# Seven modulation vectors: from plain fp32 matmuls on TensorE to sums of scaled weight rows on VectorE

## The chip, the cores and the metric

The kernel runs on one core of a Trainium2 chip. The metric is device time in microseconds (us). Before the change three runs gave a median of 3255.69 us (3248.14 to 3256.19). One further run was taken with the hardware profiler; all rows below come from it.

## The reference, cut to what matters

Two token groups, 256 context tokens and 1024 latent tokens, go through a trunk of two layers (an even mixer with attention and a linear recurrence, an odd mixer with Fourier and long-convolution branches), each followed by an MLP. Every layer is modulated by six vectors of 1024 numbers per group, which depend on a conditioning vector alone:

```
m = silu(cvec) @ mod_w[l] + mod_b[l]            # mod_w[l]: 1024 x 6144, cvec: c_ctx (context) or c (latent)
mp, ms = the six slices of m for c_ctx and for c
h = rmsnorm(x) * (1 + m[1]) + m[0];   x = x + m[2] * mixer(h)
h = rmsnorm(x) * (1 + m[4]) + m[3];   x = x + m[5] * mlp(h)      # mlp: square(relu(h @ w1)) @ w2
```

So there are 2 x 6 modulation vectors, each a product of a 2 x 1024 matrix (both groups) with a 1024 x 1024 slice of `mod_w`. All arithmetic is fp32; products that need it are built from a high and a low fp32r part of each factor (three matmuls for one).

## The kernel before, in words

Activations lie feature-major: 128 features on the partitions, 1280 tokens (256 context, 1024 latent) on the free axis, eight such tiles. The stages run one after the other: filter generation with the first modulation vectors, even mixer (projection, recurrence, attention), output projection, first MLP, odd input projection (`odd_in`), the two convolution passes (`hyena`) with the Fourier branch between, output projection, second MLP. The program is written as generators that are pulled into one another; the tile framework then orders each engine's instructions by a simulated timeline and sets the waits. Each engine works through its own list in order.

The MLP (`mlp`, L778) is a seven-product block scheme. In its first half 16 hidden tiles `j` are made; each takes seven products (`product`, L826: 24 matmuls of 128x128 by 128x320 into a pair of PSUM banks) named 11, T1, T2, 21, T3, 22, T4. Several products accumulate onto the same bank pair, and between them ScalarE copies the partial result (L855, L915, L917) or VectorE adds it to another tile (L859, L921, L925). VectorE and ScalarE split each weight tile into its high and low part (`wtile`, L794: cast on ScalarE, subtraction on VectorE, L295 inside the helper `sub`), GpSimd forms sums of weight blocks (`wset`, L806), and results go to DRAM over the SyncE queue (`keep`, L846). At the end of each hidden tile the MLP pulls its filler four times (L938). The second half (L1007 on) reads the results back and multiplies by the second weights.

Five of the twelve vectors are made outside the first MLP or not touched by the change: `modulation_pe` makes vectors 1, 0, 2, 4 and 3 of layer 0 earlier in the program. The other seven, vector 5 of layer 0 and all six of layer 1, are the filler of the first MLP (`fill2`, L1951) and are made by `modulation` (L357). For one vector it runs eight steps. A step loads two tiles `mw` of 128 x 512 fp32 over the SyncE queue (L368) and issues four matmuls (L371), each with 128x32 of the silu vector as the stationary side and 256 weight columns as the moving one, into four different groups of 32 PSUM partitions. After four steps ScalarE copies the bank to `ms` (L375). After eight, eight matmuls with a selection matrix (L379) add the four partition groups and transpose, and VectorE adds the bias (L380). An fp32 matmul stands in the trace as two records. `modulation` also yields after each step, so 63 pulls finish it within the 64 of the MLP.

Vectors 1 and 0 of layer 1 are needed for the norm in front of the odd input projection, vector 5 of layer 0 at the end of the first MLP, and vectors 2, 4, 3, 5 of layer 1 only in the output projection and the second MLP.

`odd_in` (L1468) makes 16 output tiles `i`. Each loads one weight tile over the SyncE queue (`wload`, L665: load, cast `wh` on ScalarE, subtraction `wl` on VectorE), runs 72 matmuls (`proj`, L673), scales by the norm on VectorE (`evac`, L698) and, for 12 of them, runs a three-tap convolution (one ScalarE and two VectorE passes, L1501 and L1503); 12 tiles are transposed on TensorE.

The pool `tp` holds a ring of 128 x 512 fp32 temporaries that `tmp` (L244) hands out: `mw`, `ms`, the weight sums `s1` of the MLPs, `ub` and `dg` of the projection, `win` of the filter generation, `r1` and `r2` of the rotary embedding.

## Time and profile before

| | |
|---|---|
| median of three runs | 3255.69 us |
| profiled execution | 3253.46 us |
| its span on the core | 3251.3 us |
| TensorE busy | 91% of the span |
| VectorE busy | 59% |
| ScalarE, GpSimd busy | 40%, 31% |
| granted TensorE clock, mean | 0.952 of full speed |

The span is what the trace covers; the execution is 2.2 us longer. The first half of the first MLP lies at about 781 to 1291 us, its second half up to 1702 us, the odd input projection from 1711 us to about 1945 us, and the second MLP begins at 2378 us. PE stands for TensorE, DVE for VectorE, ACT for ScalarE, POOL for GpSimd, SP for SyncE.

### The profile page before, as it was taken

To read this page: it belongs to the slowest core of one execution; us is meant where nothing else is said; L and a number is where in the kernel's file an instruction comes from. 1 tells how busy PE (TensorE), PEld (TensorE's weight loads), DVE (VectorE), ACT (ScalarE), POOL (GpSimd) and SP (SyncE) were. 2 spreads that over 40 slices of the span, in tenths; PEclk is the share of its full clock that TensorE was granted. 3 is DMA by queue.
4 is the path that set the end of the run, shared out by engine and by line. 5 is a ranking of instruction groups with operands and counts; after the bars stand their busy time and mean duration, and the time that the engine had idled before them with its cause. 6 is when DMAs were issued, how large, how long until landed. Compare 5 with 4: busy or idle time off the path is not lost. (4 is left out here: it accounts for less than half of the span.)

```text
span 3251.3 us, 47128 instructions
## 1 busy us (share of the span) xinstructions
PE 2973.1 (91%) x18846; PEld 2718.9 (84%) x18846; DVE 1914.1 (59%) x2266; ACT 1286.9 (40%) x1960; POOL 1010.6 (31%) x674
## 2 busy tenths in 40 slices
PE   6689978898899999999989997887969999999997
PEld 3577767787789988999988885667969999999997
DVE  6986788747644434554664338686585444455465
ACT  5565757733423333333343332232343333333332
POOL 3530045423332222130340015453143333222043
PEclk8799989999899999999999998888989999999998
DMA  7372332252455557785541234555413333775554
GB/s 240 106 244 90 117 122 85 72 209 82 149 175 180 182 177 268 249 288 170 172 174 41 73 99 149 198 161 187 147 63 124 140 136 134 254 265 206 192 193 138
DMA packets 177679, 524.49 MB, mean 161 GB/s; under 512 B 19810, under 2 KB 34546, under 8 KB 177460
## 3 DMA queue, kind: packets, MB, share of 16 engines
q1 hardware_dynamic: 165940, 479.54, 42.6%
q0 software_dynamic: 11520, 41.95, 4.3%
q8 instruction: 148, 2.42, 0.3%
q14 instruction: 71, 0.58, 0.1%
HBM read 392.68 MB, written 128.74 MB: 160 GB/s over the span
## 5 line engine op out<-in xcount | busy, mean ns | idle before, releaser
L1024 PE MATMUL pd<-oh,wt 128*128 128x320 f32 x3584 | 681.2, 311 | 19.1 <-ACT wt L298 8.8
L1024 PEld LDWEIGHTS pd<-oh,wt 128*128 128x128 f32 x3584 | 565.8, 189 | 25.1 <-ACT wt L298 13.2
L831 PE MATMUL pd<-BT,wt 128*128 128x320 f32 x3072 | 483.7, 313 | 12.3 <-DVE BT L761 12.2
L831 PEld LDWEIGHTS pd<-BT,wt 128*128 128x128 f32 x3072 | 459.7, 190 | 31.4 <-issue 18.1
L1024 PE MATMUL pd<-ol,wt 128*128 128x320 f32 x1792 | 410.6, 310 | 1.5 <-DVE ol L295 1.5
L295 DVE TENSOR_TENSOR wt<-wr,wt 128x512 fp32r<-128x512 f32 (+1 forms) x256 | 230.3, 901 | 301.8 <-ACT wt L797 273.7
L831 PE MATMUL pd<-B,wt 128*128 128x320 f32 x2304 | 371.8, 316 | 29.6 <-DVE u L859 17.2
L831 PEld LDWEIGHTS pd<-B,wt 128*128 128x128 f32 x2304 | 351.8, 193 | 42.2 <-DVE u L859 17.8
L295 DVE TENSOR_TENSOR ol<-ur,oh 128x1280 fp32r<-128x1280 f32 x112 | 195.1, 1743 | 246.3 <-PE pd L1024 200.5
L1024 PEld LDWEIGHTS pd<-ol,wt 128*128 128x128 f32 x1792 | 302.3, 189 | 1.9 <-DVE ol L295 1.8
L298 ACT CAST oh<-ur 128x1280 fp32r<-128x1280 f32 x112 | 141.4, 1263 | 339.4 <-DMA ur<-uscr 336.3
L684 PE MATMUL pb<-hh,wh 128*128 128x258 f32 (+1 forms) x720 | 189.7, 367 | 8.0 <-DVE xm L988 8.0
L684 PE MATMUL pb<-hl,wh 128*128 128x258 f32 (+1 forms) x720 | 195.7, 372 | 0.0
L684 PE MATMUL pb<-hh,wl 128*128 128x258 f32 (+1 forms) x720 | 191.8, 370 | 0.0
L797 ACT CAST wt<-wr 128x512 fp32r<-128x512 f32 x192 | 118.7, 620 | 170.9 <-PE pd L831 145.8
L684 PEld LDWEIGHTS pb<-hh,wh 128*128 128x128 f32 x720 | 122.5, 192 | 33.4 <-issue 13.0
L684 PEld LDWEIGHTS pb<-hl,wh 128*128 128x128 f32 x720 | 123.0, 191 | 26.3 <-issue 6.7
L684 PEld LDWEIGHTS pb<-hh,wl 128*128 128x128 f32 x720 | 122.7, 192 | 26.1 <-issue 5.8
L810 POOL TENSOR_TENSOR s<-wr 128x512 f32<-128x512 f32 x32 | 42.3, 1322 | 325.9 <-DMA wr<-in_w_dram 283.7
L306 PE MATMUL pb<-arh,tab 128*128 128x512 f32 x288 | 115.3, 426 | 25.6 <-ACT arh L298 16.2
L298 ACT CAST wh<-wr 128x1024 fp32r<-128x1024 f32 x62 | 64.9, 1048 | 158.8 <-PE pd L684 88.2
L298 ACT CAST wt<-wr 128x1024 fp32r<-128x1024 f32 x64 | 67.3, 1052 | 112.3 <-PE pd L1024 100.9
(529 smaller groups left out, 5588.2 us busy)
## 6 DMA issues: line engine op xcount, KB each, us to landing
wr<-in_w_dram SPq DMA_DIRECT2D x196, 512.0 KB, 3.7
uscr<-u SPq DMA_DIRECT2D x224, 320.0 KB, 2.4
ur<-uscr SPq DMA_DIRECT2D x112, 640.0 KB, 4.2
tab<-in_dft_dram POOLq DMA_DIRECT2D x79, 512.0 KB, 4.8
mw<-in_mw_dram SPq DMA_DIRECT2D x112, 256.0 KB, 4.3
wq<-in_w_dram SPq DMA_DIRECT2D x48, 512.0 KB, 6.2
mw<-in_mw_dram SPq DMA_DIRECT2D x40, 512.0 KB, 5.0
x<-in_x_dram SPq DMA_DIRECT2D x16, 640.0 KB, 7.7
```

Source lines behind the costliest of these rows:

```text
L295: eng.tensor_tensor(o, x, y, ALU.subtract)
L298: S.copy(hi, src)
L306: T.matmul(ps, w, m, start=(i == 0), stop=(i == n - 1))
L684: T.matmul(ps[c][:, 0:N], w[wi][:, sl], hs[k][hi][:, c0:c0 + N], start=(ki == 0 and pi == 0), stop=(ki == nk - 1 and pi == 2))
L797: S.copy(t[:, 0], src)
L810: G.tensor_tensor(s1, a21, a22, ALU.add)
L831: T.matmul(ps[:, c, 0:NQ], w[:, wi, 128 * k:128 * k + 128], B[n][k][:, hi_, NQ * c:NQ * c + NQ], start=(onto is None and k == 0 and pi == ...
L1024: T.matmul(ps[mi][:, z, 0:NQ], w[wi][:, k2, 128 * mi:128 * mi + 128], o[oi][:, k2, NQ * z:NQ * z + NQ], start=(fresh and kk == 0 and k2 == ...
```

## The change

`modulation` no longer runs the weights through TensorE. For one vector it takes two halves of 512 columns. For a half it loads eight tiles `mq` of 128 x 512 (128 rows of the weight matrix each), and for each tile and each of the two groups VectorE multiplies the tile by one number per partition (the silu value of that row) and adds it to an accumulator `macc` of 128 x 2 x 512. The first tile of a half writes the accumulator (a tensor_scalar), the other seven add (scalar_tensor_tensor). At the end of a half eight matmuls with `macc` as the stationary side and one column of ones as the moving one sum over the partitions and bring the result feature-major; VectorE adds the bias. A vector has 18 yields.

Three vectors (layer 0's 5, layer 1's 1 and 0) stay in the first MLP; the other four (layer 1's 2, 4, 3, 5) become the filler of `odd_in`, which pulls five times per output tile. The ring of temporaries shrinks from 6 to 4. The weights are packed accordingly.

```diff
-    o["mw"] = mw.reshape(2, 2, 4, 128, 24, 256).transpose(0, 4, 1, 3, 2, 5).reshape(2, 24, 2, 128, 1024)
+    o["mw"] = mw[0, :, 0:5120].reshape(2, 4, 128, 20, 256).transpose(3, 0, 2, 1, 4).reshape(20, 2, 128, 1024)
+    o["mq"] = np.concatenate([mw[0, :, 5120:], mw[1]], axis=1).reshape(8, 128, 7, 2, 512).transpose(2, 3, 0, 1, 4)
...
-    tp = root.enter_context(tc.tile_pool(name="tp", bufs=6))
+    tp = root.enter_context(tc.tile_pool(name="tp", bufs=4))
...
     def modulation(l, which):
         for i in which:
-            mss = []
-            for jj in range(2):
-                ps = tbank()
-                for h in range(2):
-                    for kk in range(2):
-                        ws = []
-                        for z in range(2):
-                            w = tmp("mw", (128, 2, 256))
-                            ld(w.rearrange("p k c -> p (k c)"), a["mw"][l, 4 * i + 2 * jj + h, kk, :, 512 * z:512 * z + 512])
-                            ws.append(w)
-                        for g in range(4):
-                            T.matmul(ps[32 * g:32 * g + 32, 256 * h:256 * h + 256], st[:, 4 * kk + g, :], ws[g // 2][:, g % 2, :],
-                                     start=kk == 0, stop=kk == 1)
-                        yield
-                ms = tmp("ms")
-                S.copy(ms, ps)
-                mss.append(ms)
-            p2 = tbank()
-            for c in range(8):
-                T.matmul(p2[:, 2 * c:2 * c + 2], mss[c // 4][:, 128 * (c % 4):128 * (c % 4) + 128], sel, start=True, stop=True)
-            V.tensor_tensor(mod[l][i], p2[:, 0:16].rearrange("p (c s) -> p c s", s=2),
-                            mb[:, l, 8 * i:8 * i + 8].unsqueeze(2).to_broadcast([128, 8, 2]), ALU.add)
-            yield
+            for hf in range(2):
+                acc = cp.tile([128, 2, 512], F32, tag="macc", name="macc")
+                for k in range(8):
+                    w = tmp("mq")
+                    ld(w, a["mq"][i + 1 if l else 0, hf, k])
+                    for z in range(2):
+                        if k:
+                            V.scalar_tensor_tensor(acc[:, z], w, st[:, k, z:z + 1], acc[:, z], ALU.mult, ALU.add)
+                        else:
+                            V.tensor_scalar(acc[:, z], w, st[:, k, z:z + 1], None, ALU.mult)
+                    yield
+                p2 = tbank()
+                for c in range(4):
+                    for z in range(2):
+                        T.matmul(p2[:, 2 * c + z:2 * c + z + 1], acc[:, z, 128 * c:128 * c + 128], ones[:, 0:1], start=True, stop=True)
+                V.tensor_tensor(mod[l][i][:, 4 * hf:4 * hf + 4, :], p2[:, 0:8].rearrange("p (c s) -> p c s", s=2),
+                                mb[:, l, 8 * i + 4 * hf:8 * i + 4 * hf + 4].unsqueeze(2).to_broadcast([128, 4, 2]), ALU.add)
+                yield
...
         for i in list(range(8)) + list(range(12, 16)) + list(range(8, 12)):
...
             ps = proj(w, 0, 128, hs, HC, order=[4, 5, 6, 7, 0, 1, 2, 3])
+            pull(filler, 5)
...
         def fill2():
             yield from modulation(0, (5,))
-            yield from modulation(1, (1, 0, 2, 4, 3, 5))
+            yield from modulation(1, (1, 0))
...
-        odd_in(n2, norm_end(n2), vt, h0)
+        fill = modulation(1, (2, 4, 3, 5))
+        odd_in(n2, norm_end(n2), vt, h0, fill)
+        drain(fill)
```

The changed file has four lines less ahead of the MLP, so its L827 is L831 of before, L368 and L370 are the new accumulations, L375 the new column sums and L376 the bias. The engines' lists move as follows.

First TensorE in the first half of the first MLP, around the place where a hidden tile's product 22 (operands `B_6875` to `B_6899`) and T4 (`BT_6878` to `BT_6902`) end and the next tile begins. Before:

```order
L831 MATMUL pd<-B_6899,wt 128x320 x6
L371 MATMUL pt<-mw,silu 32x256 x2
L831 MATMUL pd<-BT_6878,wt 128x320 x6
L831 MATMUL pd<-BT_6886,wt 128x320 x6
L831 MATMUL pd<-BT_6894,wt 128x320 x6
L831 MATMUL pd<-BT_6902,wt 128x320 x6
L371 MATMUL pt<-mw,silu 32x256 x2
L379 MATMUL pt<-c_sel,ms 128x2 x4
L831 MATMUL pd<-B_6276,wt 128x320 x6
```

And at the same place now:

```order
L827 MATMUL pd<-B_6899,wt 128x320 x6
L827 MATMUL pd<-B_6276,wt 128x320 x3
L375 MATMUL pt<-ones,macc 128x1
L827 MATMUL pd<-B_6276,wt 128x320 x3
L375 MATMUL pt<-ones,macc 128x1 x3
L827 MATMUL pd<-BT_6878,wt 128x320 x6
L827 MATMUL pd<-BT_6886,wt 128x320 x6
L827 MATMUL pd<-BT_6894,wt 128x320 x6
L827 MATMUL pd<-BT_6902,wt 128x320 x6
L375 MATMUL pt<-ones,macc 128x1 x4
```

The `mw` matmuls are gone from the list, and six times in this half of the MLP (14 times in all) eight column sums over `macc` stand among the products.

Then VectorE for one hidden tile of the same half (from the addition L859 on, L855 in the changed file). Before:

```order
L859 TENSOR_TENSOR u_8368<-u_8368,pd 128x640
L295 TENSOR_TENSOR wt<-wr,wt 128x512
L921 TENSOR_TENSOR u_8398<-u_8398,pd 128x640
L295 TENSOR_TENSOR wt<-s_8523,wt 128x512
L922 SCALAR_TENSOR_TENSOR u_8398<-u_8398 128x640
L925 TENSOR_TENSOR u_8368<-u_8368,pd 128x640
L295 TENSOR_TENSOR wt<-wr,wt 128x512
L926 SCALAR_TENSOR_TENSOR u_8368<-u_8368 128x640
L295 TENSOR_TENSOR u_8368<-u_8368 128x640
L295 TENSOR_TENSOR u_8398<-u_8398,u_8368 128x640
```

And now:

```order
L855 TENSOR_TENSOR u_8267<-u_8267,pd 128x640
L296 TENSOR_TENSOR wt<-wr,wt 128x512
L368 SCALAR_TENSOR_TENSOR macc<-mq,silu,macc 128x512 x2
L917 TENSOR_TENSOR u_8297<-u_8297,pd 128x640
L368 SCALAR_TENSOR_TENSOR macc<-mq,silu,macc 128x512
L296 TENSOR_TENSOR wt<-s_8422,wt 128x512
L368 SCALAR_TENSOR_TENSOR macc<-mq,silu,macc 128x512
L918 SCALAR_TENSOR_TENSOR u_8297<-u_8297 128x640
L921 TENSOR_TENSOR u_8267<-u_8267,pd 128x640
L296 TENSOR_TENSOR wt<-wr,wt 128x512
L922 SCALAR_TENSOR_TENSOR u_8267<-u_8267 128x640
L296 TENSOR_TENSOR u_8267<-u_8267 128x640
```

The accumulations stand singly and in pairs in front of and between the additions from PSUM (L917, L921) and the weight splits.

Last VectorE for one output tile of the odd input projection (L698 scales by the norm, L1503 is the convolution, `wl` the low part of the next weights; L694, L1500 and L296 in the changed file). Before:

```order
L698 TENSOR_TENSOR xp<-pb,R 128x512 x2
L295 TENSOR_TENSOR wl<-wr,wh 128x1024
L698 TENSOR_TENSOR xp<-pb,R 128x256
L1503 SCALAR_TENSOR_TENSOR u<-xp,hy_14657,u 128x1024
L1503 SCALAR_TENSOR_TENSOR u<-xp,hy_14657,u 128x256
```

And now:

```order
L694 TENSOR_TENSOR xp<-pb,R 128x512 x2
L368 SCALAR_TENSOR_TENSOR macc<-mq,silu,macc 128x512
L296 TENSOR_TENSOR wl<-wr,wh 128x1024
L694 TENSOR_TENSOR xp<-pb,R 128x256
L368 SCALAR_TENSOR_TENSOR macc<-mq,silu,macc 128x512 x3
L1500 SCALAR_TENSOR_TENSOR u<-xp,hy_14355,u 128x1024
L1500 SCALAR_TENSOR_TENSOR u<-xp,hy_14355,u 128x256
L1500 SCALAR_TENSOR_TENSOR u<-xp,hy_14355,u 128x1024
L1500 SCALAR_TENSOR_TENSOR u<-xp,hy_14355,u 128x256
L368 SCALAR_TENSOR_TENSOR macc<-mq,silu,macc 128x512 x8
```

Up to eight accumulations in a row now fill the place between the convolution of one tile and the scaling of the next.

## Rows read from the trace of the kernel before

**Rows 1.** The page: span, and busy time of the engines.

```profile
span 3251.3 us, 47128 instructions
PE 2973.1 (91%) x18846; PEld 2718.9 (84%) x18846; DVE 1914.1 (59%) x2266; ACT 1286.9 (40%) x1960; POOL 1010.6 (31%) x674
```

**Rows 2.** Windows: stretch, length, busy PE PEld DVE ACT POOL, clock, DMA share, GB/s.

```profile
840.00:1300.00 460.00, 456.40 (x3142) 408.65 (x3143) 187.37 (x236) 143.90 (x229) 135.39 (x92) 0.99 0.57 195
980.00:1130.00 150.00, 150.00 (x1051) 136.63 (x1050) 60.97 (x75) 48.37 (x79) 43.13 (x30) 1.00 0.53 180
1720.00:1920.00 200.00, 200.00 (x1079) 171.10 (x1078) 65.62 (x88) 69.65 (x114) 2.10 (x28) 1.00 0.20 60
2500.00:2600.00 100.00, 100.00 (x683) 100.00 (x682) 47.78 (x57) 35.32 (x56) 35.32 (x25) 1.00 0.38 135
```

**Rows 3.** Groups by line, 840 to 1300 us: count, busy us, mean ns.

```profile
L371 PE MATMUL pt<-mw,silu 128*32 128x256 f32 x448 | 55.0, 397 | 5.0 <-DMA mw<-in_mw_dram 5.0
L379 PE MATMUL pt<-c_sel,ms 128*128 128x2 f32 x112 | 13.7, 246 | 0.0
```

**Rows 4.** Timeline of TensorE, first MLP: start, length, work [idle before, releaser].

```profile
841.62 3.04 PE L371 MATMUL pt<-mw,silu 128*32 128x256 f32 x16 [5.02 <-DMA mw<-in_mw_dram]
846.37 5.19 PE L831 MATMUL pd<-B,wt 128*128 128x320 f32 x24 [1.71 <-ACT u L915]
...
1290.85 0.56 PE L1024 MATMUL pd<-oh,wt 128*128 128x320 f32 x2 [0.27 <-DVE mod L380]
```

**Rows 5.** Timeline of TensorE, the same places of the second MLP.

```profile
2443.79 5.20 PE L831 MATMUL pd<-B,wt 128*128 128x320 f32 x24 [9.76 <-ACT u L915]
...
2817.01 0.56 PE L1024 MATMUL pd<-oh,wt 128*128 128x320 f32 x2 [0.92 <-ACT u L850]
```

**Rows 6.** Timeline of TensorE, start of the odd input projection: column sums of the norm.

```profile
1726.19 2.29 PE L643 MATMUL pt<-ones,nsq 128*128 128x1 f32 x20
1728.34 0.48 PE L684 MATMUL pb<-hh,wh 128*128 128x512 f32 x1
```

**Rows 7.** Single lines on VectorE: count, duration ns min/median/max, first and last start.

```profile
L1503 DVE SCALAR_TENSOR_TENSOR u<-xp,hy,u x32: 476/1208/2300, 1796.7 to 1972.5; 128x1024 f32<-128x1024 f32 x16, 128x256 f32<-128x256 f32 x16
...
L1503 DVE SCALAR_TENSOR_TENSOR u<-xp,hys,u x8: 1543/1553/1557, 1743.9 to 1783.3; 128x1282 f32<-128x1282 f32 x8
...
L461 DVE TENSOR_SCALAR sn<-sa x6: 286/417/421, 14.1 to 34.6; 128x512 f32<-128x512 f32 x4, 128x256 f32<-128x256 f32 x2
```

**Rows 8.** Groups by line on VectorE, 840 to 1300 us.

```profile
L295 DVE TENSOR_TENSOR wt<-wr,wt 128x512 fp32r<-128x512 f32 (+1 forms) x91 | 66.9, 735 | 164.7 <-ACT wt L797 162.0 <-ACT wt L298 2.5
L922 DVE SCALAR_TENSOR_TENSOR u<-u 128x640 f32<-128x640 f32 x16 | 27.3, 1706 | 0.0
L926 DVE SCALAR_TENSOR_TENSOR u<-u 128x640 f32<-128x640 f32 x16 | 13.0, 815 | 0.1
```

**Rows 9.** Waits, 840 to 1300 us: who for whom, us in total, times, longest.

```profile
ACT wt L797 <- PE pd L831: 82.3, 37, 4.8
...
DVE mod L380 <- PE pt L379: 17.7, 5, 4.6
```

**Rows 10.** Timeline of VectorE, one output tile of the odd input projection.

```profile
1822.79 1.29 DVE L698 TENSOR_TENSOR xp<-pb,R 128x512 f32<-128x512 f32 x2 [7.72 <-PE pb L684]
1824.00 1.22 DVE L295 TENSOR_TENSOR wl<-wr,wh 128x1024 fp32r<-128x1024 f32 x1
1825.13 0.42 DVE L698 TENSOR_TENSOR xp<-pb,R 128x256 f32<-128x256 f32 x1
1827.03 3.27 DVE L1503 SCALAR_TENSOR_TENSOR u<-xp,hy,u 128x1024 f32<-128x1024 f32 x4 [1.48 <-issue]
1837.98 1.29 DVE L698 TENSOR_TENSOR xp<-pb,R 128x512 f32<-128x512 f32 x2 [7.67 <-PE pb L684]
```

**Rows 11.** The page: DMA issues of the old modulation: count, size, us to landing.

```profile
mw<-in_mw_dram SPq DMA_DIRECT2D x112, 256.0 KB, 4.3
```

**Rows 12.** Waits of ScalarE and TensorE in the filter stage, 55 to 240 us.

```profile
ACT win L509 <- DVE O L524: 8.0, 3, 3.1
...
PE pt L543 <- DVE fsq L541: 30.2, 4, 25.1
```

More of the change, by code (lines that the diff above doesn't have):

```diff
@@ L331, in modulation_pe @@
                     w = wp.tile([128, 4, 256], F32, tag=tags[n % len(tags)], name="mw")
-                (ld if len(tags) == 1 else LDM)(w.rearrange("p k c -> p (k c)"), a["mw"][0, 4 * i + 2 * jj + h, kk])
+                (ld if len(tags) == 1 else LDM)(w.rearrange("p k c -> p (k c)"), a["mw"][4 * i + 2 * jj + h, kk])
                 ws.append(w)
@@ L1465, in out_proj, with odd_in @@
         return xt
-    def odd_in(s, R, vt, h0):
+    def odd_in(s, R, vt, h0, filler):
         hs = s.h
```

## The prediction

> **What bounds the kernel now.** The page comes first: TensorE is busy for 91% of a span of 3251.3 us, VectorE for 59% [rows 1]. An average over the program does not say which engine sets the time where the change acts, so the second view is the windows. In the first half of the first MLP TensorE is busy 456.4 of 460 us, and from 980 to 1130 us all of 150 us, while VectorE has 61 us of work there; in the odd input projection TensorE is busy all of 200 us and VectorE 66 us [rows 2]. Both stages are paced by TensorE: what leaves its list there shortens the program, and what is added lengthens it, unless VectorE turns late. Third, the groups by line: the old modulation holds TensorE for 55.0 us (L371) and 13.7 us (L379) in the first MLP [rows 3]. Fourth, the kernel has a control of its own: the second MLP runs the same products with an empty filler, and there TensorE is busy 100 of 100 us too [rows 2]. So the modulation of the first MLP fills no holes in the steady state, and the second MLP shows what the stage takes without it.
>
> **The change, part by part.**
>
> *The modulation matmuls leave the first MLP.* I compare from the same place in both, the start of the hidden tile's second accumulation, to the first matmul of the second half. First MLP: 846.37 to 1290.85 us, 444.5 us [rows 4]. Second: 2443.79 to 2817.01 us, 373.2 us [rows 5]. The same 2520 product matmuls lie in both, 15 tiles' worth: 29.6 us a tile against 24.9. The difference, 71.3 us, is what the filler costs, a little over the 68.7 us of its busy time [rows 3], since products and small matmuls do not overlap perfectly where they meet. I take 71.3. The first block of modulation (3.04 us at 841.62) is left out on purpose: it stands in a hole that the second MLP has as well (9.76 us idle at the same place), so it costs nothing today and gives nothing back [rows 4, 5].
>
> *Column sums are added.* A half vector has eight matmuls of 128x128 by one column, 16 records in the trace. The nearest row is the norm's column sum, the same shape: 20 records from 1726.19 to the next product at 1728.34, 2.15 us or 0.1075 us each [rows 6]. That is 1.72 us for a half. Upper end: L379, with two columns, has 13.7 us / 112 = 0.122 us, 1.96 us for a half [rows 3]; lower end: nothing, were they all in waits, which a TensorE that is never idle excludes. I take 1.72: six halves in the first MLP, 10.3 us; eight in the odd projection, 13.8 us. Here the change adds work to TensorE that was not there.
>
> *VectorE's accumulations.* A half has 14 scalar_tensor_tensor and 2 tensor_scalar of 128x512. From L1503, the same operation with a scalar per partition and all operands in SBUF: 1553 ns for 1282 columns and 476 ns for 256, so 1.05 ns a column and, at 512, 745 ns [rows 7]. The tensor_scalar is at most the 417 ns of L461 [rows 7]. In the first MLP GpSimd works beside it, and there an equal operation takes two times: L926 815 ns, L922 1706 ns [rows 8]. So an accumulation costs between 0.745 and about 1.65 us. L922 runs each time right when GpSimd's subtractions run; the 91 weight splits, spread over the tile as the accumulations will be, have a mean of 735 ns [rows 8]. I stay near these and take 0.9 us: 84 x 0.9 + 12 x 0.42 = 81 us in the first MLP, 6 us a tile over 13.5 tiles (54 yields at four a tile). VectorE has 61 us per 150 us, 12.0 us in a tile of 29.6 [rows 2]. It comes to 18.0 us in a tile of 25.6 us, seven tenths. It keeps slack, but its list is in order: behind an accumulation that waits for its `mq` stand the additions from PSUM (L917, L921 of the new file), whose banks the next product but one wants, one product or 24.9 / 7 = 3.6 us later, and the weight splits. Those have room: ScalarE today waits 82.3 us for TensorE to give weight buffers back, so weights are made ahead [rows 9].
>
> On the lock behind L922 the Trainium skill speaks too. Its page "SBUF — State Buffer", section "Who interferes with whom", says that a VectorE instruction with two SBUF inputs and a GpSimd instruction that reads SBUF shut each other out, the later one waiting for the whole of the other. L922 against L926 agrees with it. By that rule, as an estimate, an accumulation would meet a busy GpSimd 135 times in 460 and then lose some 0.9 us: 1.0 us in the mean instead of 0.9, a tile's VectorE work 18.8 us instead of 18.0, and the sum the same; it makes rival C less likely, since C needs every accumulation held.
>
> *Waits added.* The accumulator is single, so a half's first operation waits for the column sums of the half before, which stand in TensorE's list among products. The bias add of today waits likewise, 17.7 us in five waits [rows 9], while TensorE stays full. TensorE waits in turn for the last accumulation of a half; in the new list the sums stand about a tile behind it, so VectorE must fall a tile back before they hold TensorE. At the start, accumulations stand in front of the last operands of the first tile while TensorE waits: about 1 us. I put 3 us of new waiting into the first MLP.
>
> *The odd input projection.* Per output tile VectorE has 1.29 + 1.22 + 0.42 + 3.27 = 6.2 us in a period of 15.2 us (1822.79 to 1837.98), and waits for TensorE for most of the rest [rows 10]. Five pulls bring ten operations, 7.5 us at 745 ns, since GpSimd has only 2.1 us of work in 200 [rows 2]: 13.7 us in a period of some 16 with the column sums. VectorE keeps up, with up to eight accumulations in a row ahead of the scaling and of the low part `wl`, which the next tile's third matmul group needs. I put 4 us.
>
> *Queues and DMA.* Of the 112 loads of 256 KB [rows 11] 48 remain in the first MLP, so SyncE's queue gets lighter where it carries 195 GB/s. The 64 `mq` loads of the odd projection are 16.8 MB in about 230 us, 73 GB/s beside 60, less than the first MLP carries today [rows 2]. A load waits for a place in the ring of four, and the next weight load stands behind it on SP; weights have a tile of lead, so no cost while VectorE keeps pace.
>
> *The smaller ring elsewhere.* In the filter stage `win` runs six ahead, now four. ScalarE waits there 8.0 us for VectorE and TensorE 30.2 us for sums of squares [rows 12]. Bounds: nothing, or two exponentials' lateness in each of a few steps, 8 us. I take 2. The 14 copies `ms` leave ScalarE, off the path: nothing.
>
> *Sum.* 3251.3 - 71.3 + 10.3 + 13.8 + 3 + 4 + 2 = 3213.1 us of span; with the 2.2 us that the execution has around it, 3215 us. The profiled execution, 3253.5 us, lies 2.2 us under the median of the runs, well within their spread.
>
> **The rivals.**
>
> *A, all waits hidden.* Both stages stay paced by TensorE and the smaller ring costs nothing: 3251.3 - 71.3 + 10.3 + 13.8 + 2.2 = 3206 us. For it: seven tenths and nine tenths load. Against: in-order lists with single accumulator.
>
> *B, VectorE late in the odd projection.* At 0.9 us instead of 0.745 the ten operations make 9.0 us and VectorE 15.2 us a tile, no slack left; what it is late with then comes out at `wl`, before each projection. 1.5 us for each of 14 tiles is 21 us: 3232 us, and up to 3246 when the first MLP adds some. For it: the long rows of accumulations. Against: GpSimd idle there.
>
> *C, slower.* In the first MLP every accumulation takes L922's time: 7.1 a tile x 1.9 us + 12.0 = 25.5 us, all of the tile's 25.6. VectorE is then never early, and two hand-offs from PSUM a tile come about 2 us late each, 4 us x 15 = 60 us: 3251.3 - 71.3 + 24.1 + 60 + 6 + 2.2 = 3272 us. It turns into a loss when the first MLP waits over 41 us more, 2.7 us a tile. Against it: the splits' mean of 735 ns and that only L922 of the evenly spread operations is slow.
>
> *D, it gives back less.* Were part of the modulation today in hidden waits, as its first block is, half of 71.3 us would be gained: about 3250 us. Against: the full windows of the second MLP.
>
> **How the numbers follow.** My forecast, 3209 to 3225 us around 3215, has 0.50; A 0.22; B 0.14; D 0.06; C 0.08. Faster or slower by over 0.3% (what can be told from no change) means under 3246 or over 3265 us. So faster 0.50 + 0.22 + 0.13 = 0.85, same 0.07 (D and the edge of B), slower 0.08. The range reaches from 3203 (A with cheaper sums) to 3246, leaving out C, D and the edges.
>
> **What would show it.** Right: no TensorE records of 32 output rows in the first MLP; its first half from the same place to the second half in 384 to 390 us; column sums of about 1.7 us; accumulations of 0.75 us in the odd projection and under 1.1 us in the MLP; TensorE at 97% or more in both; VectorE at some 70% and 85%. Wrong: TensorE waiting for `u` additions or `wt` in the first MLP (C), for `wl` or `macc` in the odd projection (B), or more than 5 us later at the end of the filter stage.

## The result and the profile after

The changed kernel takes 3206.76 us (median of 4 runs, 3205.85 to 3208.13) against 3251.91 us of the kernel before beside it (4 runs, 3245.22 to 3256.19): ratio 0.9863, 95% interval 0.9842 to 0.9884, faster by 1.4%. Forecast were 3215 us, rival A stood at 3206. From the page of the changed kernel:

```profile
span 3203.3 us, 46668 instructions
PE 2916.2 (91%) x18510; PEld 2710.5 (85%) x18510; DVE 2089.7 (65%) x2497; ACT 1279.3 (40%) x1946; POOL 1039.4 (32%) x674
```

TensorE's share is still 91% of a shorter span; VectorE went from 59% [rows 1] to 65%. Where the time went is seen from the places that the prediction measured between: in the timeline of TensorE of the changed kernel the fixed place of the first MLP and the first matmul of its second half answer to [rows 4].

```profile
840.13 1.44 PE L827 MATMUL pd<-BT,wt 128*128 128x320 f32 x4 [8.43 <-ACT wt L793]
843.22 6.14 PE L827 MATMUL pd<-B,wt 128*128 128x320 f32 x24 [1.66 <-ACT u L911]
...
1229.16 0.56 PE L1020 MATMUL pd<-oh,wt 128*128 128x320 f32 x2 [0.79 <-ACT u L846]
```

1229.2 - 843.2 = 386.0 us, against 444.5 before. The windows of that first half and of the whole odd input projection (columns as in [rows 2]):

```profile
843.20:1229.20 386.00, 383.24 (x2613) 382.72 (x2613) 259.10 (x312) 130.38 (x207) 139.35 (x86) 0.99 0.49 175
1654.80:1915.30 260.50, 260.50 (x1427) 224.70 (x1428) 177.51 (x260) 82.12 (x133) 22.57 (x49) 0.99 0.42 132
```

TensorE is full in both, VectorE has 67% and 68%. The odd projection took 245.9 us before and 260.5 now. These two stages make -58.5 + 14.6 = -43.9 us of the -48.0 us between the two spans; the other stages (among them the first MLP up to the fixed place, 1.8 us longer, and its second half, 5.5 us longer) differ by up to 5.5 us each, in both directions, and sum to -4.1. In the 14 profiles of this study the stage up to the first MLP took 772 to 785 us, with no order by kernel, so single stages are compared below and not whole spans. Two numbers of the new work, the lines of the accumulator on VectorE (count, ns min/median/max, first and last start) and one run of column sums on TensorE:

```profile
L368 DVE SCALAR_TENSOR_TENSOR macc<-mq,silu,macc x196: 734/746/2061, 839.9 to 1895.4; 128x512 f32<-128x512 f32 x196
L370 DVE TENSOR_SCALAR macc<-mq,silu x28: 474/482/1514, 835.6 to 1880.9; 128x512 f32<-128x512 f32 x28
```

```profile
1705.46 1.84 PE L375 MATMUL pt<-ones,macc 128*128 128x1 f32 x16
1707.17 0.36 PE L680 MATMUL pb<-hh,wh 128*128 128x258 f32 x1
```

The 16 records begin at 1705.46 and the next product at 1707.17: 1.71 us, where 1.72 was taken from [rows 6]. (Most half-vectors' sums stand in two or three pieces with products between, 2 and 14 records for instance; the pieces add up to the same.)

### The profile page after: what moved, and what is told of

Its sections match the earlier page's. It is cut to its first block, busy times and chain, and to the rows that moved or that the text cites. A ratio compares the mean times of both kernels' runs of the same rounds, so it can differ in the third digit from the quotient of the medians.

```text
span 3203.3 us, 46668 instructions
## 1 busy us (share of the span) xinstructions
PE 2916.2 (91%) x18510; PEld 2710.5 (85%) x18510; DVE 2089.7 (65%) x2497; ACT 1279.3 (40%) x1946; POOL 1039.4 (32%) x674
## 3 DMA queue, kind: packets, MB, share of 16 engines
q1 hardware_dynamic: 165940, 479.54, 43.1%
## 5 line engine op out<-in xcount | busy, mean ns | idle before, releaser
L1020 PEld LDWEIGHTS pd<-oh,wt 128*128 128x128 f32 x3584 | 564.0, 189 | 29.5 <-ACT wt L299 14.6
L827 PE MATMUL pd<-BT,wt 128*128 128x320 f32 x3072 | 475.9, 312 | 21.6 <-DVE BT L757 11.2
L827 PEld LDWEIGHTS pd<-BT,wt 128*128 128x128 f32 x3072 | 460.2, 190 | 22.8 <-DVE BT L757 11.7
L827 PE MATMUL pd<-B,wt 128*128 128x320 f32 x2304 | 371.0, 316 | 31.0 <-DVE u L855 17.8
L827 PEld LDWEIGHTS pd<-B,wt 128*128 128x128 f32 x2304 | 354.2, 194 | 33.7 <-DVE u L855 18.3
L296 DVE TENSOR_TENSOR ol<-ur,oh 128x1280 fp32r<-128x1280 f32 x112 | 201.3, 1798 | 255.8 <-PE pd L1020 194.1
L296 DVE TENSOR_TENSOR wt<-wr,wt 128x512 fp32r<-128x512 f32 (+1 forms) x256 | 236.7, 928 | 186.6 <-ACT wt L793 166.1
L368 DVE SCALAR_TENSOR_TENSOR macc<-mq,silu,macc 128x512 f32<-128x512 f32 x196 | 162.1, 866 | 23.0 <-DMA mq<-in_mq_dram 23.0
L680 PEld LDWEIGHTS pb<-hh,wl 128*128 128x128 f32 x720 | 123.1, 191 | 26.6 <-issue 6.7
L307 PE MATMUL pb<-arh,tab 128*128 128x512 f32 x288 | 114.6, 424 | 24.1 <-ACT arh L299 16.7
```

The lines of the kernel that those rows point to most:

```text
L296: eng.tensor_tensor(o, x, y, ALU.subtract)
L307: T.matmul(ps, w, m, start=(i == 0), stop=(i == n - 1))
L368: V.scalar_tensor_tensor(acc[:, z], w, st[:, k, z:z + 1], acc[:, z], ALU.mult, ALU.add)
L680: T.matmul(ps[c][:, 0:N], w[wi][:, sl], hs[k][hi][:, c0:c0 + N], start=(ki == 0 and pi == 0), stop=(ki == nk - 1 and pi == 2))
L827: T.matmul(ps[:, c, 0:NQ], w[:, wi, 128 * k:128 * k + 128], B[n][k][:, hi_, NQ * c:NQ * c + NQ], start=(onto is None and k == 0 and pi == ...
L1020: T.matmul(ps[mi][:, z, 0:NQ], w[wi][:, k2, 128 * mi:128 * mi + 128], o[oi][:, k2, NQ * z:NQ * z + NQ], start=(fresh and kk == 0 and k2 == ...
```

## The experiments

Theory T is the sum of the prediction: TensorE paces both stages, the old form cost 71.3 us, a half-vector's column sums cost 1.72 us, VectorE keeps up. The stages of every run, in us, from its timeline (start: first product of the first MLP to the fixed place; half 1: from there to the second half; odd: the odd input projection; waits: TensorE's in half 1, with the one before the first product of the second half, 0.3 to 2.4 us). Every stage comes from one profiled execution, every median from 4 to 10 runs; the ratios are against runs of the kernel before beside each run.

```
kernel        median    start  half 1  odd    waits
before        3251.9    65.7   444.5   245.9   0.3
after         3206.8    67.6   386.0   260.5   2.7
e1_none       3169.9    65.7   373.4   246.5   0.8
e2_nosums     3189.2    67.6   378.6   246.3   5.2
e3_move       3255.1    65.7   401.4   289.9   0.8
e4_all7       3248.5    67.5   439.7   247.1  26.9
e5_ring4      3267.2    65.5   459.3   246.1   5.5
e7_extra      3214.2    67.6   386.2   258.4   2.8
e8_sums2      3258.5    67.6   404.2   289.7   2.7
e9_all7b      3233.6    72.6   421.5   245.9  15.4
e10_fine      3209.4    71.8   383.3   260.4   0.8
e11_split     3243.6    72.6   394.1   288.0   0.8
e12_late      3207.8    65.5   385.8   260.2   2.8
e13_latefine  3209.8    67.6   386.3   261.4   3.0
```

**e1_none: the seven products left out** (only the bias is written).

```diff
-                    w = tmp("mq")
-                    ld(w, a["mq"][i + 1 if l else 0, hf, k])
...
-                            V.scalar_tensor_tensor(acc[:, z], w, st[:, k, z:z + 1], acc[:, z], ALU.mult, ALU.add)
...
-                        T.matmul(p2[:, 2 * c + z:2 * c + z + 1], acc[:, z, 128 * c:128 * c + 128], ones[:, 0:1], start=True, stop=True)
```

> Leaves out the seven vectors' products: no weight loads, no accumulations, no column sums; the bias alone is written in their place. Theory T (TensorE paces both stages; the change costs only its column sums and a few us of waits): the first half of the first MLP takes 373 to 375 us from its fixed place (changed kernel 385.9), the odd projection 246 us (260.5), the time is 24.1 us of column sums and 2 to 4 us of waits below the changed kernel's 3206.8, so 3179 us. Rival R1 (VectorE's accumulations slow the stages through in-order waits and the port shared with GpSimd): over 35 us below, under 3172 us.

3169.89 us, ratio 0.9748 (0.9733 to 0.9762). Half 1 takes 373.4 us, what the second MLP takes (373.2, [rows 5]), and the odd projection 246.5: the two stages are as T has them. The total, 36.9 us below the changed kernel, meets R1's figure and not T's 3179. But only 26.6 us of that lie in the two stages. In the profiles the start gives 1.9 us, which e12_late below shows to be the accumulations' doing; the rest comes from stages the edit doesn't touch (before the first MLP 3.6 us less than in the changed kernel, its second half 3.0 less), of which no run shows a cause. So R1's mechanism is there in small, some 4 us, and not at the size that it named. The old form did cost 444.5 - 373.4 = 71.1 us; the new one costs 12.6 and 14.0.

**e2_nosums: loads and accumulations stay, the column sums are left out** (the bias is added to a part of the accumulator instead).

```diff
-                for c in range(4):
-                    for z in range(2):
-                        T.matmul(p2[:, 2 * c + z:2 * c + z + 1], acc[:, z, 128 * c:128 * c + 128], ones[:, 0:1], start=True, stop=True)
```

> Leaves out the column sums alone: loads and accumulations stay, the bias add reads the accumulator directly. T: nearly the time of the run without any of it, 3182 us, first half of the first MLP 375 us, odd projection 246 to 248 us, though VectorE has 170 us more work than there. R1: the accumulations are the cost, so it stays within 10 us of the changed kernel, 3197 us or more.

3189.24 us (3183.06 to 3196.99), ratio 0.98 (0.9779 to 0.9821). The odd projection is back at 246.3 us: its 14.2 us are the eight column sums and nothing else. Half 1 takes 378.6, of which 5.2 are waits, 4.2 for VectorE's `u`; without them it is close to e1_none. In the changed kernel it takes 7.4 us more with 2.7 us of waits: the sums fill part of them. The total lies between T's 3182 and R1's 3197 and decides nothing: its four runs spread over 14 us, and the profiled one, the slowest, took 9 us longer up to the first MLP than the changed kernel's.

**e3_move: the old matmul form, four vectors moved.** The kernel before, with vectors 2, 4, 3, 5 pulled in the odd projection.

```diff
-            yield from modulation(1, (1, 0, 2, 4, 3, 5))
+            yield from modulation(1, (1, 0))
...
+            pull(filler, 3)
...
+        fill = modulation(1, (2, 4, 3, 5))
+        odd_in(n2, norm_end(n2), vt, h0, fill)
```

> The move alone: the old matmul form on TensorE, but four of the seven vectors are made in the odd projection. T: the matmuls cost TensorE the same there: first half of the first MLP 373 + 3/7 x 71 = 404 us, odd projection 246 + 4/7 x 71 = 287 us, time within 6 us of the kernel before. Rival R2 (the gain comes from taking loads and work out of the busy first MLP, not from the form): 15 us or more faster than before, under 3238 us.

3255.06 us, ratio 1.0013 (1.0003 to 1.0022). Half 1 loses 43.1 us and the odd projection grows by 44.0. Moving alone is worth nothing, since TensorE is full at both places; it is the form that gains, 10.2 us a vector before and 3.8 now ((12.6 + 14.0) / 7).

**e4_all7: the new form, not moved**, all seven vectors in the first MLP, none in the odd projection.

```diff
-            yield from modulation(1, (1, 0))
+            yield from modulation(1, (1, 0, 2, 4, 3, 5))
...
-            pull(filler, 4)
+            pull(filler, 8)
```

> The form alone: all seven vectors as VectorE sums, all in the first MLP, eight pulls a hidden tile. T: TensorE still paces: first half of the first MLP 373 + 14 x 1.72 = 397 us and some 5 us of waits, odd projection 246 us, time 3207 to 3215 us. VectorE has 12 us of its own and 14 operations of about 0.85 us a tile, 24 of 26.5 us. R1: VectorE becomes the pace, 2 us a tile late or more: over 3235 us.

3248.54 us, ratio 0.9991 (0.9977 to 1.0005): the gain is gone, and T's figure for half 1 fell (439.7 us). The window, TensorE's waits there, and two short windows (stretch, length, TensorE busy, clock, DMA share, GB/s) of e4_all7:

```profile
846.50:1286.20 439.70, 412.68 (x2740) 407.69 (x2740) 358.12 (x456) 132.15 (x208) 141.26 (x86) 0.97 0.57 195
```

```profile
PE pd L827 <- DVE u L917: 12.4, 9, 2.9
PE pt L375 <- DVE macc L368: 12.3, 8, 4.7
PE pd L827 <- DVE wt L296: 1.5, 1, 1.5
```

```profile
1136.30:1146.30 10.00, 10.00 (x71) 1.00 0.63 193
...
1156.30:1166.30 10.00, 8.52 (x39) 0.66 0.48 159
```

VectorE has 358 of 440 us, 81%, and is late at two hand-offs that the prediction named: the additions from PSUM (L917, rival C) and the last accumulation of a half, which the column sums in TensorE's list wait for (under *Waits added*). A second price comes with it: the granted clock of five stretches of 10 us is 0.83 (four) or 0.66, each with waits of TensorE of 0.7 to 2.7 us in it or at its start, and in all but one the column sums stand right behind them. 0.83 means that TensorE had 1.2 GHz instead of 2.4 for a third of the stretch, which costs 1.7 us. 373.4 + 24.1 (sums) + 26.2 (waits) + 10.2 (clock) = 434 of the 439.7 us. (A sixth stretch, the last of the half, has 0.76 behind a wait of 4.7 us; its 16 sums take 3.8 us instead of 1.8.) So the split between two stages is a part of the gain.

**e9_all7b: the same with the steps spread**, two pulled at each of four places of a tile instead of eight at its end (one of the three new places is shown, against e4_all7).

```diff
+            pull(filler, 2)
             product("T3", nextw(), x)
...
-            pull(filler, 8)
+            pull(filler, 2)
```

> All seven vectors in the first MLP as in the run before (439.7 us for the first half, 26.9 us of it waits of TensorE), but the 8 steps of a tile are pulled 2 at a time at four places of the tile instead of 8 in one burst. Theory T (it was the burst of 16 accumulations of 0.98 us in a row, ahead of VectorE's own work for the tile, that made TensorE wait): the first half at 398 to 415 us, the whole at 3210 to 3228 us. Rival R1 (it is VectorE's load, 358 of 440 us with its instructions lengthened by the transfers and GpSimd beside it, wherever the work stands): the first half at 430 to 442 us, the whole at 3238 to 3252 us. Rival R2 (TensorE's wait at the column sums, 12.3 us in 8 times, is what is left): the first half at 415 to 430 us with the waits on the sums' input at 10 us or more.

3233.58 us, ratio 0.9953 (0.9938 to 0.9968). Half 1 takes 421.5: waits 15.4 instead of 26.9, four stretches of 10 us at a low clock. It lies in R2's band, but with 4.4 us at the column sums' input and 8.6 at L917, so R2's reason is not what is left. The spread takes 18.2 us off half 1 and puts 5.0 on the start: 13 of the 42 us by which e4_all7's half 1 lies above 373.4 + 24.1. So bursts were less than half of the trouble. The rest goes with VectorE's load, 353 of 422 us here, but no run changed that load alone; what it would have to be for no waits at all is open.

**e5_ring4: only the ring**, the kernel before with four buffers.

```diff
-    tp = root.enter_context(tc.tile_pool(name="tp", bufs=6))
+    tp = root.enter_context(tc.tile_pool(name="tp", bufs=4))
```

> The kernel before with one thing changed: the ring of shared load tiles has 4 buffers instead of 6, the matmul form of the modulation stays. Theory T (the prediction's term: the smaller ring costs about 2 us in the filter stage, and nothing that the new form gains comes from it): 3251 to 3256 us, the first MLP's first half at 444 to 450 us, the first MLP starting at 780 to 785 us. Rival R1 (the 5 us by which the changed kernel reached the first MLP earlier come from the ring): the first MLP starts at 774 to 777 us and the time is 3244 to 3248 us. Rival R2 (the old form needs the six buffers, its tiles are loaded in pairs): the first half goes to 455 us or more and the time above 3262 us.

3267.19 us, ratio 1.0048 (1.0031 to 1.0065): slower, as R2 has it. The first MLP starts at 779.1 us (780.6 before), so neither the 2 us of the prediction nor R1's gain can be seen in it. ScalarE does wait longer for places of `win` in the filter stage (55 to 240 us, the line of [rows 12] and that of e5_ring4):

```profile
ACT win L509 <- DVE O L524: 8.0, 3, 3.1
ACT win L509 <- DVE O L524: 11.3, 4, 5.2
```

Half 1 grows by 14.8. In e5_ring4 TensorE waits once for a load, and the same 432 records of L371 hold it longer (the fixed place to the second half; first the wait and the records of e5_ring4, then those of the kernel before):

```profile
PE pt L371 <- DMA mw<-in_mw_dram: 4.6, 1, 4.6
L371 PE MATMUL pt<-mw,silu 128*32 128x256 f32 x432 | 58.2, 392 | 4.6 <-DMA mw<-in_mw_dram 4.6
L371 PE MATMUL pt<-mw,silu 128*32 128x256 f32 x432 | 52.0, 388 | 0.0
```

The wait and the 6.2 us are 10.8 of the 14.8.

The smaller ring hurts the form that is removed, whose TensorE waits itself for its tiles. The new form puts that wait on VectorE, which has the slack: in half 1 of the changed kernel

```profile
DVE macc L368 <- DMA mq<-in_mq_dram: 15.9, 10, 2.6
```

The new form with six buffers was not run.

**e7_extra: VectorE loaded more in the odd projection** (56 more accumulations; the vectors are changed by it).

```diff
+                            if l and i > 1 and z:
+                                V.scalar_tensor_tensor(acc[:, z], w, st[:, k, z:z + 1], acc[:, z], ALU.mult, ALU.add)
```

> The changed kernel with one accumulation more in every step of the four vectors in the odd input projection (its first operand used twice, so the result is not the reference's): 64 more accumulations less the first of each half-vector, 56 to 64 at 0.746 us, 42 to 48 us more work for VectorE in that stage. Theory T (VectorE is not late there, TensorE's column sums are the whole cost): VectorE busy 219 to 226 of about 261 us, the stage at 259 to 266 us, the whole at 3204 to 3212 us. Rival B of the prediction (a burst of accumulations makes VectorE late for the tiles that TensorE waits for): the stage at 271 us or more, the whole at 3217 us or more, with waits of TensorE on VectorE's u or on the column sums' input.

3214.22 us (3210.31 to 3217.04), ratio 0.9884 (0.9869 to 0.9899). The stage stays at 258.4 us, with VectorE at 206.5, less than T has. The rest of the work went elsewhere, as the line of the added accumulations (first and last start) shows:

```profile
L370 DVE SCALAR_TENSOR_TENSOR macc<-mq,silu,macc x56: 733/745/1986, 1686.6 to 1961.0; 128x512 f32<-128x512 f32 x56
```

The projection ends at 1916.4: the accumulations run 45 us into the next stage. That stage, up to the first product of the output projection, takes 286.3 us, the longest of all runs (277.3 to 284.9 in the others, 280.9 in the changed kernel), and behind the projection's end TensorE waits for the accumulations, in a place where the changed kernel has no such wait:

```profile
PE pt L377 <- DVE macc L368: 4.1, 1, 4.1
```

In the changed kernel the last accumulation starts at 1895.4, 20 us before the end of the projection. So rival B doesn't come about in the stage even with this load: what is too much for VectorE runs over its end and holds TensorE there. How much of the 7.5 us between the two medians that wait makes isn't shown. The total lies between T's band and B's.

**e8_sums2: every column sum issued twice.**

```diff
+                        for again in range(2):
+                            T.matmul(p2[:, 2 * c + z:2 * c + z + 1], acc[:, z, 128 * c:128 * c + 128], ones[:, 0:1], start=True, stop=True)
```

> The changed kernel with each matmul of the column sums issued twice into the same place. Theory T (a half-vector's sums cost 1.72 us of TensorE's time, all of it on the path in both stages, so 14 more cost 24.1 us): the first MLP's first half at 394 to 398 us (386.0 before the doubling), the odd input projection at 273 to 276 us (260.5), the whole at 3227 to 3234 us. Rival R1 (the sums are partly covered by waits that would be there anyway, as the first half's 7.4 us between the kernel without sums, 378.6, and with them suggests): the first half at 389 to 393 us and the whole at 3218 to 3226 us.

3258.46 us, ratio 1.0019 (1.0007 to 1.0032): twice the price that T has, +18.2 us in half 1 and +29.2 in the odd projection, and neither theory. In e8_sums2 the first of the runs of 32 in the odd projection, and the windows over it and behind it:

```profile
1728.15 3.63 PE L376 MATMUL pt<-ones,macc 128*128 128x1 f32 x32
```

```profile
1726.40:1736.40 10.00, 10.00 (x61) 9.00 (x60) 7.34 (x11) 6.03 (x9) 0.16 (x3) 0.83 0.26 79
1736.40:1746.40 10.00, 10.00 (x57) 8.61 (x56) 10.00 (x13) 3.13 (x6) 0.17 (x3) 1.00 0.35 108
```

And the window over the run of 16 shown above, in the changed kernel:

```profile
1704.90:1714.90 10.00, 10.00 (x62) 8.83 (x61) 8.78 (x13) 5.87 (x9) 0.16 (x3) 1.00 0.35 106
```

In this run of 32 a record costs the same as in the run of 16 (3.49 us from the run to the next product). The rest goes with the clock: 0.83 in a stretch that holds a run of 32, 1.00 in one with 16. In the odd projection the clock falls so at all eight doubled sums. In half 1, where products split them, the longest pieces are of 22 to 32 records; behind four of the six (28, 22, 32, 22) it falls, behind two (28, 26) it stays at 1.00.

**e11_split: the same doubled sums, cut in two** in the first MLP (16 and 16, with products between; the steps are pulled one at a time at four places of a tile, as in e10_fine below), but still 32 in a row in the odd projection, where four of a tile's five pulls now stand before its products.

```diff
+                for z in range(2):
+                    if z:
+                        yield
+                    for c in range(4):
+                        for again in range(2):
...
-            pull(filler, 4)
+            pull(filler)
```

> The column sums issued twice, as before (404.2 us for the first half, the granted clock at 0.57 to 0.95 in eight stretches of 5 us behind four of the six long runs of column sums), but with the sums of the two output vectors asked for at two places of the first MLP's tile, so that in the program's order of TensorE they stand there as 16 records and 16, three to five runs of matmuls apart; in the odd input projection they still stand as 32 in a row. Theory T (the clock falls behind a run of 32 short records and not behind 16, so only the records themselves, 1.72 us per 16, are left where the run is cut): the first half at 394 to 399 us with its clock at 0.99, the odd input projection still at 286 to 291 us with its clock at 0.93, the whole at 3242 to 3254 us. Rival R1 (it is the number of records in all, however cut): the first half at 402 to 406 us with its clock at 0.97. Rival R2 (the clock doesn't matter, a record in a long run simply takes longer): the first half at 394 to 399 us with a clock that still falls.

3243.57 us, ratio 0.9981 (0.9969 to 0.9993). The windows of half 1 and of the odd projection in e11_split:

```profile
847.70:1241.80 394.10, 393.21 (x2708) 392.81 (x2708) 261.68 (x308) 129.93 (x206) 136.57 (x86) 1.00 0.47 170
1665.00:1953.10 288.10, 288.07 (x1523) 249.41 (x1524) 176.53 (x259) 82.54 (x133) 17.15 (x49) 0.93 0.38 120
```

Where the runs are cut the clock stays at 1.00 and half 1 is 394.1 us; where they aren't it is 0.93 and the stage nearly as long as in e8_sums2. T holds, both rivals fall. The control with the same pulls and no doubling is e10_fine, 383.3 us: the doubling costs 10.8 us, 1.8 for each half-vector.

**e10_fine, e12_late, e13_latefine: can the rest be had?** In the changed kernel the first accumulations stand in front of the MLP's start, 67.6 us instead of 65.7. e12_late begins them at the second tile, e10_fine pulls them singly, e13_latefine does both. The edit of e12_late:

```diff
-            pull(filler, 4)
+            if j:
+                pull(filler, 4)
```

> The changed kernel with the accumulations of the first MLP beginning at its second tile instead of its first (no pull at tile 0; 15 tiles at 4 steps still hold the 54). In the changed kernel two plain products and a first sum (2.74 and 1.75 us) stand in VectorE's row before the last input of the fixed place, TensorE waits 8.43 us there on a weight cast and reaches the place 67.5 us after the MLP's first matmul, against 65.7 without the accumulations; the granted clock of the 10 us behind it is 0.74 against 0.84. Theory T: this is the accumulations' doing, so the start goes back to 65.5 to 66.0 us, the clock behind it to 0.83 to 0.85, the first half to 384 to 386 us, and the whole to 3202 to 3205 us (-2 to -4). Rival R1 (something else of the change, the ring of 4, makes the start late): the start stays at 67.5 us and the time within 1 us of 3206.8.

> The changed kernel with the 4 steps of a first-MLP tile pulled one at a time at four places of the tile instead of together at its end. Theory T (bursts cost the changed kernel next to nothing, since its waits in the first half are 2.7 us in all): the first half at 384 to 387 us and the whole within 3 us of 3206.8. Rival R1 (the earlier places let the first accumulations get in front of the MLP's start still more, as in the run with seven vectors and fine pulls, whose start took 72.5 us): the start at 69 to 73 us and the whole at 3208 to 3213 us.

> The changed kernel with both last edits: the steps of the first MLP begin at its second tile and are pulled one at a time at four places of a tile. Theory T (the two gains are independent: the late begin gives the start back its 1.8 to 2 us, the single pulls shorten the first half by 2.6 us): the start at 65.5 to 66.0 us, the first half at 382.5 to 384 us, the two together at 448 to 450 us against 453.4 in the changed kernel, the whole at 3200 to 3205 us if the stages that the edit doesn't touch are as they were there. Rival R1 (the single pulls of the second tile move the accumulations in front of the MLP's start again): the start at 67 us or more and the two together at 452 us or more.

e12_late brings the start back to 65.5 us, as T has it; e10_fine shortens half 1 to 383.3 and lengthens the start to 71.8, as its R1 has it; together they give neither (67.6 and 386.3, R1). e12_late's total misses T's 3202 to 3205; its profiled execution took 9 us longer up to the first MLP than the changed kernel's. The medians are 3207.8 (3200.9 to 3214.5), 3209.4 and 3209.8 us, ratios 0.9875, 0.9879 and 0.9869, whose intervals overlap that of the changed kernel: no version beats it by what can be measured.

## Why the prediction held, and which terms were off

- *The old form leaves, -71.3 us.* Right: 71.1 us, shown by e1_none. The second MLP was a good control. Rival D falls.
- *Column sums, +10.3 and +13.8.* Right: 14.2 us for the eight of the odd projection (e2_nosums); for the six of the first MLP 9.9 us (e10_fine against e1_none, neither with waits in half 1 before its last 0.8 us). That they are at 1.72 us rests on runs of 16 and shorter; the eight doubled sums of e8_sums2 cost 29.2 us more in the odd projection, twice the price, which nothing in the trace of before shows.
- *Accumulations.* In the odd projection the mean is 746 ns, the forecast 745. The tensor_scalar takes 482 ns there and 731 in the first MLP, above the 417 that I took for the most (a median: the most in [rows 7] is 421). In the first MLP the accumulation's mean is 1020 ns for the 0.9 us of the prediction:

```profile
L368 DVE SCALAR_TENSOR_TENSOR macc<-mq,silu,macc 128x512 f32<-128x512 f32 x82 | 81.9, 1020 | 15.9 <-DMA mq<-in_mq_dram 15.9
```

  The trace says why. Of the 84 accumulations of the first MLP 46 overlap no instruction of GpSimd and take 734 to 743 ns; the 38 that overlap one take 1371 in the mean. The weight splits that I stayed near were a poor neighbour: only 8 of 91 overlap GpSimd in the trace of before. The transfers, which R1 of e9_all7b names too, don't show: in that run the 130 accumulations of half 1 without GpSimd beside them take 739 ns in the mean, at 199 GB/s. GpSimd is longer as well; its subtraction in half 1 of e1_none, without accumulations, and of the changed kernel:

```profile
L296 POOL TENSOR_TENSOR u<-u,u 128x640 f32<-128x640 f32 x15 | 23.9, 1590 | 59.6 <-DVE u L296 56.1 <-DVE u L906 3.5
L296 POOL TENSOR_TENSOR u<-u,u 128x640 f32<-128x640 f32 x15 | 29.6, 1976 | 99.5 <-DVE u L296 92.0 <-DVE u L918 7.5
```

  1.0 us is what the estimate by the Trainium skill's page "SBUF — State Buffer", section "Who interferes with whom", gave. The trace agrees with the mean, in part by luck: the estimate has three in ten accumulations meet GpSimd and lose 0.9 us, the trace has 45% lose 0.63.
- *Waits in the first MLP, +3.* Right in size: half 1 is 386.0 in the forecast's 384 to 390, with 1.9 us of waits that the kernel without the products doesn't have, and the start is 1.8 us longer, which e12_late shows to be the accumulations. C didn't come about at three vectors; e4_all7 shows that late additions from PSUM are real at seven, at half of C's accumulation time (0.98 us in the mean instead of 1.9).
- *Waits in the odd projection, +4: this step failed.* TensorE waits for nothing new there; the only wait of the changed kernel's stage is that of its first operands, 8.0 us, as before:

```profile
PE pb L680 <- DVE xm L984: 8.0, 1, 8.0
```

  The prediction counted ten operations in each tile and 85% for VectorE; over the stage it has 68%. VectorE does stand still for the column sums (22.7 us in 7 waits for L375 before the bias add), without making TensorE late. e7_extra adds over 40 us more, 29 of which run in the stage at no cost to it.
- *The smaller ring in the filter stage, +2: open.* The wait that the term is made of is there: 3.3 us more of ScalarE for `win` in e5_ring4. Whether TensorE comes later by it can't be told: the first MLP starts 1.5 us earlier than before, in a stage that differs by 13 us among the 14 profiles.
- *The sum.* It starts at the profiled 3253.5 us and takes off 38.2; the medians show 45.1, from 3251.9. So of the 8.5 us between 3215.3 and the time, 1.6 are the base and 6.9 the gain. Of these the 4 us of waits in the odd projection are the failed term; the 2 of the ring can't be told; the rest is under the spread. Rival A's 3206 leaves out the 3 us of the first MLP as well and lies nearest. Its claim, all waits hidden, holds in the odd projection and not quite in the first MLP. That its total fits to 1 us is in part luck, since the stages outside the two differ by -4.9 to +5.5 us. The largest of them is the second half of the first MLP, which no term touches: 425.6 us against 420.1, and 423 to 428 in nearly all runs of the new form against 420 to 423 in the others. TensorE waits 15.6 us in it instead of 11.5, 2.2 of the difference for weight casts. What makes them so wasn't tried.

## What to carry to other kernels

Work that moves from a full engine to one with slack gave, in this kernel, its whole time on the first less what it must still leave there (here 26.6 of 71.1 us), as long as the receiving engine's list had room: in the first MLP three vectors at 67% load cost about 4 us of waits and later start, seven at 81% gave all of the gain back. The share alone does not decide: in the odd projection 79% (e7_extra) held TensorE up by nothing in the stage and by 4.1 us behind it. Spread such work over stages before spreading it within one, and look for its overload behind the stage as well as in it. Before taking a neighbour's mean for the price of an operation, count how often each meets the other engine. Keep runs of very short matmuls short, and put longer products between them.

## What was not expected of the hardware

- TensorE's granted clock fell from 1.00 to 0.83 over a stretch of 10 us that holds a run of 32 one-column fp32 matmul records (3.6 us), with TensorE busy all 10 us: a third of it at 1.2 GHz instead of 2.4. It did not over runs of 16 (1.8 us) nor, in e11_split, over 16 and 16 with products between. In half 1 of e8_sums2 the mean is 0.97 and in e11_split, with as many records, 1.00. The 14 extra sums cost 47 us instead of 24. The length of the run is not the whole of it: in half 1 of e8_sums2 the clock fell behind two runs of 22 and stayed at 1.00 behind one of 26 and one of 28. What decides there is not shown.
- Waits of TensorE of 0.7 to 2.7 us, most of them right before such sums, go with it too: in e4_all7 the low clock costs 10 us beside 26 us of waits. A single wait of 1.9 us in the changed kernel left the clock at 1.00. No run took the waits apart from the sums.
- An accumulation of 128 x 512 in fp32 takes 734 to 743 ns in the first MLP where no GpSimd instruction overlaps it, and up to 2061 ns where one does.
